# A hybrid decoder block on one core: raw weight tiles kept between the half turns of w_down, four segments, a start in 512-wide loads, and a new order

## The chip, the cores and the metric

The kernel runs on one core of a Trainium2 chip. The metric is the device time of one execution in microseconds (us); lower is better. The kernel before takes 1189.65 us, the median of 3 runs (1189.48 to 1189.77). The engines are TensorE (PE, matmuls), VectorE (DVE), ScalarE (ACT), GpSimd (POOL) and SyncE (SP, which issues the weight loads).

## The reference

One decoder block over 256 tokens of width 2048, all in float32: a modulation from a vector c, attention and a gated short convolution beside each other, an output projection, and a gated feed-forward network (FFN) with a convolution of three taps along the tokens. The change touches the FFN (h2 is the normalised, modulated x):

```
h2 = modulate(rms_norm(x, norm2_g[l]), sh2, sc2)
u = causal_dwconv(h2 @ w_ffn_up[l], ffn_conv_w[l], ffn_conv_b[l])
u_gate, u_up = jnp.split(u, 2, axis=-1)
ffn = (jax.nn.silu(u_gate) * u_up) @ w_ffn_down[l]
x = x + g2[:, None, :] * ffn
```

w_ffn_up is 2048 x 11264 and w_ffn_down is 5632 x 2048. The modulation also needs the gate g2, from c and the last 2048 columns of w_ada.

## The kernel before

**Slots.** The program is a row of 232 slots. A slot is one load of weights into a `raw` tile (128 x 2048 float32, 1 MB, six buffers), its split into two rounded halves, hi (ACT, line 341, `split_hi`) and lo (DVE, line 350, `split_lo`, raw minus hi), and PE's matmuls with both. Each product is made as hi x hi + hi x lo + lo x hi. When lo is made, the raw tile is free, and `load_next` issues the next load on SP's queue, in a fixed order. There are three hi and three lo tiles, and the split runs two slots ahead of PE (`la`). Slots 0 to 47 are the input projection, 48 to 63 the output projection, 64 to 231 the FFN.

**Up slots.** The 11264 columns of w_ffn_up are 44 units u of 256 columns; an even u is the gate's, an odd u the up part's, and units 2g and 2g + 1 make the 22 groups g. A unit has two slots of 8 x 128 rows each (`up_slot`, 32 matmuls, two banks of PSUM `z`). Slots 64 to 75 are the first halves of units 0 to 11. Their loads are 256 columns wide (1 KB rows). After a half, ACT copies and DVE adds the sums out of `z` into `ub` (lines 860 and 870). After the second half come the three taps: ACT scales (lines 890 and 892), and DVE adds (line 900), or POOL adds by an accumulating DMA (`dma_tap`, line 905, for the taps listed in `dma_taps`). Then silu, the product (line 915), and its halves gh and gl (lines 919 and 923).

**Down slots.** Groups 0 to 17 go through w_ffn_down by a scheme of seven products for a 2 x 2 block, in place of eight. The 2048 columns are two parts fp of 1024. For each group and part, an `r` slot makes three of the products from three of the four blocks of the raw tile (0.75 MB, two DMAs, lines 1038 and 1039), and a `T` slot the other four (1 MB, line 1035); ahead of a T slot's split, DVE makes sums of blocks in place (lines 360 and 363, `sums_of`). So each weight tile is loaded twice, three quarters of it the first time. The groups are cut into segments (`segs`: 4, 4, 4, 4, 2). In each segment, the `r` slots of a part are one turn and the `T` slots another; a turn adds up in three or four banks `q`, and at its end ACT copies them out (line 962) and POOL adds them to sums in DRAM by accumulating DMAs (line 964). At the end the sums are read back (`load_q`, line 978), joined on DVE (line 989, tiles l0.. for part 0 and l1.. for part 1), multiplied by g2 and added to x. Groups 18 to 21 follow directly, in the eight slots of the tail (224 to 231, banks `m('D', ...)`).

**Order.** The order of slots 76 to 223 on PE is the table `plan` ('0r1' is segment 0, r, part 1; a number is the next half of that unit). The order on the other engines comes from a planner in the program (from line 1623): a list of operations with costs, due times, tables of shifts and biases, and counts of free tiles. It picks operations one after another by its own clock. The chip then runs each engine's queue in that order, and an operation waits only for its data and buffers. The 16 tiles of w_ada for g2 are consumed on DVE between the slots (`g2at`).

Of the kernel before, what the change touches and what calls it, by code (L numbers as in the profile page):

```python
# [65 lines left out]
 'shift': {76: -5, 77: 1, 78: 9, 79: 10, 80: -3, 82: -6, 83: 1, 84: 6, 85: -2, 86: -3, 87: -9, 88: -14, 89: 5, 90: -7, 92:  # L66
# [18 lines left out]
 'bias': {'conv': -3, 'usa': 10, 'gate': 8, 'sum': 2, 'st': -47, 'lo': -27, 'ghi': -26, 'join': 3, 'glo': -3, 'evac': -3,  # L85
          'g2': 29, 'silu': 57},
# [6 lines left out]
 'segs': [4, 4, 4, 4, 2, 4],  # L93
 'join': [-70.0, -15],
 'tiles': 15,
 'early': 1.0,
 'spare': 4,
 'free0': 6,
 'spread': [[43, 0], [38, 1], [41, 1], [36, 1]],
# [19 lines left out]
 'gate': [41, 91, 23, 203],  # L119
# [48 lines left out]
 'direct': 2,  # L168
# [18 lines left out]
def tile_block(  # L187
# [108 lines left out]
    def arrive(issue):  # L296

        clock["DMA"] = max(clock["DMA"], clock["now"] + 1.5) + 2.7
        landed[issue] = clock["DMA"] + 1.5
# [29 lines left out]
    kind, held, ready_w = {}, {}, {}  # L329
# [17 lines left out]
    def split_lo(i=None):  # L347
        t, hi, nk, i = halfway.pop(0) if i is None else halves_of.pop(i)
        lo = half_tile("lo", i)
        V.tensor_tensor(out=lo[:, :nk], in0=t[:, :nk], in1=hi[:, :nk].bitcast(F32), op=ALU.subtract)  # L350
# [608 lines left out]
    def evac_q(seg, fp, n):  # L959
        if True:  # L960
            e = t2k(f"e{fp}{n}")
            act(e, qb.pop((seg, fp, n)), AF.Copy, scale=-1.0 if n in ("a", "c00", "c10") else 1.0)
# [68 lines left out]
    def down_load(k, f, nk):  # L1031
        def issue(t):
# [14 lines left out]
    def down_slot(seg, what, fp):  # L1047

        ga, gb = SEGS[seg]
        g = turn_at.get((seg, what, fp), ga)  # L1050
        turn_at[seg, what, fp] = g + 1
        first, last = g == ga, g == gb - 1
        assert g < gb
# [10 lines left out]
        i = len(slots)  # L1064
        kind[i], uses_g[i] = what, [g]
        nk = 3 if what == "r" else 4
        slots.append((down_load(2 * g, 2 * fp, nk), nk, go, 2.05 if what == "r" else 2.73, nk if first else 0))
# [3 lines left out]
    up_at = {}  # L1071

    def up_slot(u, one):
# [5 lines left out]
        def go(hi, lo):  # L1079
# [4 lines left out]
            if one:  # L1084
                for j, ft in order:
                    for w, v in ((hi, 0), (lo, 0), (hi, 1)):
                        mm(zp[u][ft][:, :256], w[:, j, ft * P:(ft + 1) * P], h2T[k + j][:, v * 256:v * 256 + 256],
                           start=begins and j == 0 and w is hi and not v, stop=ends and j == 7 and v == 1)
                return
# [18 lines left out]
        slots.append((up_load(u, k), 4, go, 5.76 if one else 5.55, 2 if begins else 0))  # L1108
        if ends:
            if i < F0 - 1:  # L1110
                at(i + 1, up_sum, u, one)
            else:
                ups.append((i, u, one, k == 8))

    def up_load(u, k):
        def issue(t):
            c = u % 2 * DFF + u // 2 * 256
            nc.sync.dma_start(t.rearrange("p a b -> p (a b)").rearrange("p (k f) -> p k f", k=8),
                              w_up[0, k * P:(k + 8) * P, c:c + 256].rearrange("(k p) f -> p k f", p=P))
        return issue  # L1120
# [9 lines left out]
    for u in range(NS):  # L1130
# [748 lines left out]
```

## Time and profile before

| | us |
|---|---|
| median of 3 runs | 1189.65 |
| profiled execution | 1195.88 |
| its span, first to last instruction | 1194.1 |
| mean granted PE clock in it | 0.985 |

The profiled execution is a single one and 6 us longer than the median of the runs; durations and waits below are taken from it. A row of a timeline gives the start, the length, the engine, line and operation, what it writes and reads, the number of instructions in it, and in brackets the idle time ahead of it and what ended that. A row of waits gives the waiting engine and line, what it waited for, then the total in us, the number of times and the longest. A row of groups gives the number of instructions, then busy time and mean ns of one, then idle time ahead of them.

### The profile page before, as it was taken

The page shows a single profiled execution, that of the slowest core. Times are in us where ns is not written, and L with a number is a line of the kernel's source. Part 1 is how long each engine was busy: PE and PEld are TensorE (multiplying, and loading weights), DVE is VectorE, ACT ScalarE, POOL GpSimd, SP SyncE. Part 2 cuts the span into 40 slices and gives each one's busy share as a digit, 9 for nine tenths or more (in the row PEclk, how much of TensorE's full clock was granted, in tenths as well). Part 3 has the DMA queues.
Part 4 walks back from the last instruction along what each step waited for, and adds up shares of the span by engine and source line. Part 5 has one row for each costly group of instructions (what it writes and reads, how often), then busy time and mean ns, then how long its engine had stood idle before and what let it go on. Part 6 is the DMA issues. An engine that isn't in the chain of part 4 may idle for free. (4 is left out here: it accounts for less than half of the span.)

```text
span 1194.1 us, 15939 instructions
## 1 busy us (share of the span) xinstructions
PE 1142.1 (96%) x5897; PEld 955.9 (80%) x5897; DVE 1062.7 (89%) x1153; ACT 781.4 (65%) x1187; POOL 116.7 (10%) x145
## 2 busy tenths in 40 slices
PE   7999999999999999799999999999999999997897
PEld 4767788888888888688888877878888787886776
DVE  4889989999999979899999989799999788985776
ACT  5644364668785554569886588577768776785641
POOL 2000000000000000002100011111011200131222
PEclk9999999999999999899999999999999999998899
DMA  9999989998798899899987999989889989999977
GB/s 364 408 412 390 410 333 388 378 375 313 281 331 309 292 363 335 298 307 312 306 267 271 323 347 318 312 262 336 287 259 283 311 274 307 294 265 272 305 216 144
DMA packets 205806, 374.86 MB, mean 314 GB/s; under 512 B 8464, under 2 KB 113636, under 8 KB 201376
## 3 DMA queue, kind: packets, MB, share of 16 engines
q1 hardware_dynamic: 185008, 339.63, 79.8%
q0 software_dynamic: 19280, 31.93, 13.9%
q10 hardware_dynamic: 1440, 2.29, 0.6%
q8 instruction: 46, 0.75, 0.2%
q14 instruction: 32, 0.26, 0.1%
HBM read 343.70 MB, written 23.59 MB: 308 GB/s over the span
## 5 line engine op out<-in xcount | busy, mean ns | idle before, releaser
L341 ACT ACTIVATE hi<-raw 128x2048 fp32r<-128x2048 f32 (+1 forms) x231 | 426.0, 1849 | 223.9 <-DMA raw<-in_w_in_dram 53.4
L350 DVE TENSOR_TENSOR lo<-raw,hi 128x2048 fp32r<-128x2048 f32 (+1 forms) x231 | 506.4, 2202 | 30.3 <-ACT hi L341 29.7
L1100 PE MATMUL z<-h,hi 128*128 128x512 f32 x1376 | 330.8, 393 | 7.3 <-DVE h L796 4.5
L1100 PEld LDWEIGHTS z<-h,hi 128*128 128x128 f32 x1376 | 256.0, 190 | 60.3 <-issue 4.9
L420 DVE SCALAR_TENSOR_TENSOR ada<-raw,csil,ada 128x512 f32<-128x512 f32 (+3 forms) x167 | 195.4, 1175 | 3.4
L1103 PEld LDWEIGHTS z<-h,lo 128*128 128x128 f32 x1376 | 178.0, 194 | 17.5 <-DVE lo L350 9.1
L1103 PE MATMUL z<-h,lo 128*128 128x256 f32 x1376 | 181.3, 286 | 9.3 <-DVE lo L350 7.2
L890 ACT ACTIVATE tap<-ub,fc 128x256 f32<-128x256 f32 x176 | 76.2, 501 | 3.5 <-DMA q<-e 3.3
L860 ACT ACTIVATE ub<-z 128x256 f32<-128x256 f32 x112 | 36.3, 376 | 51.6 <-PE z L1100 48.3
L360 DVE TENSOR_TENSOR raw<-raw 128x1024 f32<-128x1024 f32 x36 | 43.9, 1219 | 23.5 <-DMA raw<-in_w_ffn_down_dram 23.5
L892 ACT ACTIVATE uy<-ub,fc 128x256 f32<-128x256 f32 x88 | 47.9, 596 | 18.8 <-DVE ub L870 14.4
L1062 PE MATMUL qc<-lo,gh 128*128 128x512 f32 x108 | 43.0, 398 | 12.8 <-DVE lo L350 12.8
L363 DVE TENSOR_TENSOR raw<-raw 128x512 f32<-128x512 f32 x72 | 49.5, 690 | 1.8
L396 POOL MEMSET ada<- 128x2048 f32 x2 | 3.6, 1811 | 470.1 <-DVE lo L350 307.0
L900 DVE TENSOR_TENSOR uy<-tap,uy 128x508 f32<-128x508 f32 (+1 forms) x63 | 42.3, 684 | 7.3 <-DMA uy<-tap 5.8
L905 POOL DMA_DIRECT2D uy<-tap x25 | 30.1, 1206 | 171.9 <-ACT tap L890 107.6
L870 DVE TENSOR_TENSOR ub<-z,ub 128x256 f32<-128x256 f32 x108 | 40.5, 416 | 6.0 <-ACT ub L860 6.0
L1060 PE MATMUL qc<-hi,gl 128*128 128x512 f32 x108 | 42.2, 390 | 0.0
L1061 PE MATMUL qc<-hi,gh 128*128 128x512 f32 x108 | 42.2, 390 | 0.0
L1062 PEld LDWEIGHTS qc<-lo,gh 128*128 128x128 f32 x108 | 20.4, 189 | 19.4 <-DVE lo L350 15.4
L543 PE MATMUL mx<-hi,h 128*128 128x512 f32 x64 | 25.7, 401 | 1.2 <-ACT ada L466 1.2
L543 PE MATMUL mg<-hi,h 128*128 128x512 f32 x64 | 25.5, 399 | 0.0
(519 smaller groups left out, 1966.6 us busy)
## 6 DMA issues: line engine op xcount, KB each, us to landing
raw<-in_w_ada_dram SPq DMA_DIRECT2D x96, 1024.0 KB, 7.7
raw<-in_w_ffn_up_dram SPq DMA_DIRECT2D x88, 1024.0 KB, 8.0
raw<-in_w_in_dram SPq DMA_DIRECT2D x47, 1024.0 KB, 7.6
raw<-in_w_ffn_down_dram SPq DMA_DIRECT2D x44, 1024.0 KB, 8.0
raw<-in_w_ffn_down_dram SPq DMA_DIRECT2D x36, 512.0 KB, 5.6
raw<-in_w_out_dram SPq DMA_DIRECT2D x16, 1024.0 KB, 5.3
raw<-in_w_ffn_down_dram SPq DMA_DIRECT2D x36, 256.0 KB, 5.9
q<-e POOLq DMA_DIRECT2D x30, 256.0 KB, 8.9
```

Of the source, the lines that this page charges most:

```text
L341: act(hi[:, :nk], t[:, :nk], AF.Copy)
L350: V.tensor_tensor(out=lo[:, :nk], in0=t[:, :nk], in1=hi[:, :nk].bitcast(F32), op=ALU.subtract)
L360: V.tensor_tensor(out=t[:, 1::2], in0=t[:, 1:3], in1=t[:, 3:4].to_broadcast([P, 2, 512]), op=ALU.add)
L363: V.tensor_tensor(out=t[:, a], in0=t[:, a], in1=t[:, b], op=ALU.add)
L420: V.scalar_tensor_tensor(out=self.acc, in0=t[:, j, :], scalar=csil[:, i:i + 1], in1=self.acc, op0=ALU.mult, op1=ALU.add)
L543: mm(o, a, hi[:, k, s], start=(first and k == 0), stop=False)
L890: act(y, v, AF.Copy, scale=fcols[2 - d][:, i:i + 1])
L892: act(y, v, AF.Identity, bias=fcols[3][:, i:i + 1], scale=fcols[2][:, i:i + 1])
L900: V.tensor_tensor(out=pair(y)[:, :, d:], in0=pair(uz.pop((u, d)))[:, :, :256 - d], in1=pair(y)[:, :, d:], op=ALU.add)
L1062: mm(qb[seg, fp, n], x, lo[:, b], start=False, stop=last)
L1100: mm(zp[u][ft], hi[:, j, ft * P:(ft + 1) * P], h2T[k + j], start=begins and j == 0, stop=ends and j == 7)
L1103: mm(zp[u][ft][:, :256], lo[:, j, ft * P:(ft + 1) * P], h2T[k + j][:, :256], start=False, stop=False)
```

## The change

1. **Kept tiles.** `keep_raw` names, for each segment and part, how many of its last groups keep their raw tile between the r slot and the T slot: 2, 1, 3, 1, 2, 0, 0, 3, twelve in all. There, the r slot loads the whole tile in one DMA, and the T slot loads nothing; the raw buffer is not free until the T slot's lo is made. T turns run through their groups in falling order now.
2. **Segments.** Four (4, 4, 6, 4 groups) instead of five.
3. **Start.** Slots 64 to 75 take units in twos: a tile is 4 x 128 rows of 512 columns (2 KB rows), two units with the same g parity, and a pair of slots makes the first halves of both. Four banks are held over two slots instead of two over one.
4. **Order.** Another `plan`, `dma_taps`, `g2at`, and tables of shifts and biases; the planner's costs are changed. Its matmul slots that begin an up unit may have their lo 3.4 us late by its clock. One tap more is on DVE, and one fewer on POOL.

```diff
- 'segs': [4, 4, 4, 4, 2, 4],
- 'join': [-70.0, -15],
- 'tiles': 15,
+ 'segs': [4, 4, 6, 4, 4],
+ 'join': [-52.0, -203],
+ 'tiles': 16,
+ 'keep_raw': [2, 1, 3, 1, 2, 0, 0, 3],
...
-        load_next()
+        if i in keeps:
+            held[i] = t
+        else:
+            load_next()
...
-            held[i] = take(slots[i][0])
+            held[i] = held.pop(opener[i]) if i in opener else take(slots[i][0])
...
+        g = ga + n if what == "r" else gb - 1 - n
...
+        keep = g >= gb - CFG["keep_raw"][2 * seg + fp]
...
+        if keep and what == "r":
+            keeper[g, fp] = i
+            keeps.add(i)
+        elif keep:
+            opener[i] = keeper[g, fp]
+        slots.append((None if i in opener else down_load(2 * g, 2 * fp, 4 if keep else nk), nk, go, 2.05 if what == "r" else 2.73,
+                      nk if first else 0))
...
+    def start_slots(grp, one):
+        us = [4 * (grp // 2) + grp % 2 + w for w in (0, 2)]
+        for k in (0, 4):
+            def go(hi, lo, k=k):
...
+            slots.append((w_load(w_up, k, 4, [(grp % 2 * DFF + grp // 2 * 512, 512)]), 4, go,
+                          5.76 if one else 5.55, 4 if k == 0 else 0))
```

The first place is the end of SP's queue, from the last r loads to the tail. Lines 1038 and 1039 before (1041 and 1042 after) are the two DMAs of an r slot, 1035 (1038) a whole tile of w_down, 1118 (1161) an up load, 316 the tail's loads. Before:

```order
L1038 DMA raw<-in_w_ffn_down_dram 128x1024
L1039 DMA raw<-in_w_ffn_down_dram 128x512
L1038 DMA raw<-in_w_ffn_down_dram 128x1024
L1039 DMA raw<-in_w_ffn_down_dram 128x512
L1118 DMA raw<-in_w_ffn_up_dram 128x8x256 x3
L1035 DMA raw<-in_w_ffn_down_dram 128x2x1024
L1118 DMA raw<-in_w_ffn_up_dram 128x8x256
L1035 DMA raw<-in_w_ffn_down_dram 128x2x1024
L1118 DMA raw<-in_w_ffn_up_dram 128x8x256 x3
L1035 DMA raw<-in_w_ffn_down_dram 128x2x1024 x2
L1118 DMA raw<-in_w_ffn_up_dram 128x8x256
L316 DMA raw<-in_w_ffn_down_dram 128x4x512 x8
```

And after:

```order
L1041 DMA raw<-in_w_ffn_down_dram 128x1024
L1042 DMA raw<-in_w_ffn_down_dram 128x512
L1161 DMA raw<-in_w_ffn_up_dram 128x8x256
L1038 DMA raw<-in_w_ffn_down_dram 128x2x1024 x2
L1161 DMA raw<-in_w_ffn_up_dram 128x8x256 x2
L1038 DMA raw<-in_w_ffn_down_dram 128x2x1024
L1161 DMA raw<-in_w_ffn_up_dram 128x8x256 x4
L1038 DMA raw<-in_w_ffn_down_dram 128x2x1024 x4
L1161 DMA raw<-in_w_ffn_up_dram 128x8x256 x3
```

Before, every T slot has a load of its own (line 1035). After, the first whole tiles (x2) belong to the r slots 205 and 206, whose T slots load nothing; the single one after them is the only T load of part 1 in that segment, and the four (x4) are those of part 0, which keeps none there.

The second place is DVE's queue near slot 222, with the first join of part 1 (l1c, l), the lo of the next slots, and the gate's product and gl of groups 18 and 19. Before:

```order
L915 TENSOR_TENSOR uy_9284<-uy_9284,uy_9715 128x512
L350 TENSOR_TENSOR lo<-raw,hi 128x2048 x2
L923 TENSOR_TENSOR gl_9971<-uy_9284,gh_9964 128x512
L989 TENSOR_TENSOR l1c_9864<-l1c_9864,l1a 128x512
L989 TENSOR_TENSOR l_9862<-l_9862,l1a 128x512
L870 TENSOR_TENSOR ub_9989<-z_0_9669,ub_9989 128x256
L870 TENSOR_TENSOR ub_9989<-z_1_9670,ub_9989 128x256
L900 TENSOR_TENSOR uy_9910<-tap,uy_9910 128x2x254
L350 TENSOR_TENSOR lo<-raw,hi 128x2048
```

And after:

```order
L350 TENSOR_TENSOR lo<-raw,hi 128x2048
L992 TENSOR_TENSOR l1c_9594<-l1c_9594,l1a 128x512
L992 TENSOR_TENSOR l_9592<-l_9592,l1a 128x512
L350 TENSOR_TENSOR lo<-raw,hi 128x2048
L918 TENSOR_TENSOR uy_9162<-uy_9162,uy_9681 128x512
L350 TENSOR_TENSOR lo<-raw,hi 128x2048
L926 TENSOR_TENSOR gl_9940<-uy_9162,gh_9895 128x512
```

Before, the join stands behind the lo of slot 222, and part 1's last T slot is 217; after, it stands behind the lo of slot 221, and that T slot is 212.

The third place is DVE's queue at the join of part 0 (l0c, l), some ten rows later, with the ub and the taps of unit 43, the last. Before:

```order
L870 TENSOR_TENSOR ub_10124<-z_0_9869,ub_10124 128x256
L870 TENSOR_TENSOR ub_10124<-z_1_9870,ub_10124 128x256
L900 TENSOR_TENSOR uy_10003<-tap,uy_10003 128x2x254
L350 TENSOR_TENSOR lo<-raw,hi 128x2048
L900 TENSOR_TENSOR uy_10136<-tap,uy_10136 128x2x255
L900 TENSOR_TENSOR uy_10136<-tap,uy_10136 128x2x254
L989 TENSOR_TENSOR l0c_10087<-l0c_10087,l0a 128x512
L989 TENSOR_TENSOR l_10085<-l_10085,l0a 128x512
L350 TENSOR_TENSOR lo<-raw,hi 128x2048
```

And after:

```order
L350 TENSOR_TENSOR lo<-raw,hi 128x2048
L992 TENSOR_TENSOR l0c_9892<-l0c_9892,l0a 128x512
L992 TENSOR_TENSOR l_9890<-l_9890,l0a 128x512
L873 TENSOR_TENSOR ub_10037<-z_0_9901,ub_10037 128x256
L873 TENSOR_TENSOR ub_10037<-z_1_9902,ub_10037 128x256
L350 TENSOR_TENSOR lo<-raw,hi 128x2048
L903 TENSOR_TENSOR uy_10048<-tap,uy_10048 128x2x255
L903 TENSOR_TENSOR uy_10048<-tap,uy_10048 128x2x254
```

The join stood behind unit 43's ub and taps and ahead of the lo of slot 227, with part 0's last T slot at 222; now it stands ahead of unit 43's ub and of the lo of slot 226, with that T slot at 220.

More of the change, by code (lines that the diff above doesn't have):

```diff
@@ L296, in arrive @@
     def arrive(issue):
-        clock["DMA"] = max(clock["DMA"], clock["now"] + 1.5) + 2.7
+        clock["DMA"] = max(clock["DMA"], clock["now"] + 1.5) + getattr(issue, "us", 2.98)
         landed[issue] = clock["DMA"] + 1.5
@@ L1049, in down_slot @@
         ga, gb = SEGS[seg]
[L1050 to L1053, printed above, removed]
+        n = turn_at.get((seg, what, fp), 0)
+        turn_at[seg, what, fp] = n + 1
+        g = ga + n if what == "r" else gb - 1 - n
+        first, last = n == 0, n == gb - ga - 1
+        assert n < gb - ga
         def go(hi, lo):
@@ L1064, in down_slot, with up_slot @@
         i = len(slots)
+        keep = g >= gb - CFG["keep_raw"][2 * seg + fp]
         kind[i], uses_g[i] = what, [g]
         nk = 3 if what == "r" else 4
-        slots.append((down_load(2 * g, 2 * fp, nk), nk, go, 2.05 if what == "r" else 2.73, nk if first else 0))
+        if keep and what == "r":
[5 more added lines that the diff above has]
+                      nk if first else 0))
         if last:
             outs.extend((i, seg, fp, n) for n, *_ in FORM[what])
-    up_at = {}
-    def up_slot(u, one):
+    up_at, begin_at = {}, set()
+    def up_slot(u):
         k = up_at.get(u, 0)
@@ L1083, in go @@
             order = [(j, ft) for j in range(8) for ft in range(2)]
[L1084 to L1089, printed above, removed]
             wide = [e + (1,) for e in order]
@@ L1107, in up_slot @@
         up_slots.append((i, u))
-        slots.append((up_load(u, k), 4, go, 5.76 if one else 5.55, 2 if begins else 0))
+        if k == 0 and u >= NS:
+            begin_at.add(i)
+        slots.append((up_load(u, k), 4, go, 5.55, 2 if begins else 0))
         if ends:
+            ups.append((i, u, False, True))
+    def start_slots(grp, one):
+        us = [4 * (grp // 2) + grp % 2 + w for w in (0, 2)]
+        for k in (0, 4):
+            def go(hi, lo, k=k):
+                if k == 0:
+                    for u in us:
+                        zp[u] = [bank(f"z{u}_{ft}") for ft in range(2)]
+                z = zp[us[0]] + zp[us[1]] if us[0] in zp else None
+                parts = [(hi, 0), (lo, 0), (hi, 1)]
+                order = [(j, ft) for j in range(4) for ft in range(4)]
+                if one:
+                    run = [(0, ft, *e) for e in parts for ft in range(4)]
+                    run += [(j, ft, *e) for j in range(1, 4) for ft in range(4) for e in parts]
+                    for j, ft, w, v in run:
+                        mm(z[ft][:, :256], w[:, j, ft * P:(ft + 1) * P], h2T[k + j][:, v * 256:v * 256 + 256],
+                           start=k == 0 and j == 0 and w is hi and not v, stop=k == 4 and j == 3 and v == 1)
+                    return
+                wide = [e + (1,) for e in order]
+                low = [e + (0,) for e in order]
+                for j, ft, w in (wide + low if k == 0 else low + wide):
+                    if w:
+                        mm(z[ft], hi[:, j, ft * P:(ft + 1) * P], h2T[k + j], start=k == 0 and j == 0, stop=k == 4 and j == 3)
+                    else:
+                        mm(z[ft][:, :256], lo[:, j, ft * P:(ft + 1) * P], h2T[k + j][:, :256], start=False, stop=False)
+            i = len(slots)
+            slots.append((w_load(w_up, k, 4, [(grp % 2 * DFF + grp // 2 * 512, 512)]), 4, go,
+                          5.76 if one else 5.55, 4 if k == 0 else 0))
+        for u in us:
+            up_at[u] = 8
             if i < F0 - 1:
@@ L1129, in tile_block @@
     seven |= set(range(SEGS[-1][0]))
-    for u in range(NS):
-        up_slot(u, u < CFG["direct"])
+    for grp in range(NS // 2):
+        start_slots(grp, grp < CFG["direct"])
     for e in CFG["plan"]:
         if isinstance(e, int):
-            up_slot(e, False)
+            up_slot(e)
         else:
@@ L1137, in tile_block @@
     assert all(up_at[u] == 16 for u in range(44))
-    assert all(turn_at[n, w, fp] == SEGS[n][1] for n in range(len(SEGS) - 1) for w in "rT" for fp in range(2))
+    assert all(turn_at[n, w, fp] == SEGS[n][1] - SEGS[n][0] for n in range(len(SEGS) - 1) for w in "rT" for fp in range(2))
     LAST = len(slots)
@@ L1620, in tile_block, with __init__ @@
                 lo_of([j])
-    clock.update(PE=0.0, ACT=0.0, DVE=0.0, SP=0.0, POOL=0.0, DMA=0.0, now=0.0)
+    clock.update(PE=0.0, ACT=0.0, DVE=0.0, SP=0.0, POOL=0.0, DMA=8.0, now=0.0)
     ops = []
     class Op:
-        def __init__(self, e, cost, f, deps=(), due=1e9, need=(), free=(), lat=0.1, key=None, out=0, nb=0.0, tag=None, at=None):
+        def __init__(self, e, cost, f, deps=(), due=1e9, need=(), free=(), lat=0.1, key=None, out=0, nb=0.0, tag=None, at=None, soft=None):
             self.e, self.cost, self.f, self.deps, self.due = e, cost, f, [d for d in deps if d], due
@@ L1708, in tile_block @@
                 raw = None
[L1709 to L1710 removed]
+            hi_op[j] = Op("ACT", (1.41 if nk == 3 else 1.81 * nk / 4) + 0.02, lambda j=j: split_hi(slots[j][1], gated.get(j), j), d, key=raw, tag="hi", at=j)
+            lo_op[j] = Op("DVE", 1.79 if nk == 3 else 2.2 * nk / 4 + 0.01, lambda j=j: split_lo(j), [hi_op[j], pe.get(j - N_HL)], tag="lo", at=j)
         for g, r, *q in extra.get(i, []):
@@ L1733, in tile_block @@
                 free[q] = free.get(q, 0) + n
-        pe[i] = prev["pe"] = Op("PE", cost, lambda i=i: run_slot(i), d, due=tid[i + 1], need={"b": slots[i][4] + more}, free=free, lat=0.2)
+        soft = {}
+        if i in begin_at and lo_op.get(i):
+            soft[lo_op[i]] = 3.4
+            d.append(hi_op[i])
+        pe[i] = prev["pe"] = Op("PE", cost, lambda i=i: run_slot(i), d, due=tid[i + 1], need={"b": slots[i][4] + more}, free=free, lat=0.2, soft=soft)
         if more:
@@ L1823, in tile_block @@
                 continue
-            start = max([clock[o.e], o.nb] + [d.end + (0.05 if d.e != o.e else -1.0 if d.e == "PE" else 0.0) for d in o.deps] + [sorted(res[k])[n - 1] for k, n in o.need.items() if n]
+            start = max([clock[o.e], o.nb] + [d.end + (0.05 if d.e != o.e else -1.0 if d.e == "PE" else 0.0) - o.soft.get(d, 0.0) for d in o.deps] + [sorted(res[k])[n - 1] for k, n in o.need.items() if n]
                         + ([landed.get(o.key, 0.0)] if o.key is not None else []))
```

52 lines of the change are left out of this document (26 added, 26 removed), and 52 rows, old and new, of the table CFG.

## The prediction

> **What bounds the kernel now.** The page's busy shares come first, then the list of what TensorE (PE) waited for from 430 us on.
>
> ```profile
> PE 1142.1 (96%) x5897; PEld 955.9 (80%) x5897; DVE 1062.7 (89%) x1153; ACT 781.4 (65%) x1187; POOL 116.7 (10%) x145
> PE qc L1062 <- DVE lo L350: 12.8, 6, 8.0
> PE z L1103 <- DVE lo L350: 7.2, 4, 4.6
> PE z L1100 <- DVE h L796: 4.5, 1, 4.5
> PE z L1100 <- DVE ub L870: 2.6, 1, 2.6
> PE m('D', -1, 0)0_10094 L533 <- DVE gl L923: 2.3, 1, 2.3
> PE z L1103 <- ACT h L811: 2.1, 2, 1.6
> PE m('D', -1, 3)0_10339 L535 <- DVE lo L350: 1.7, 1, 1.7
> PE qa L1062 <- DVE lo L350: 1.2, 1, 1.2
> PE z L1100 <- ACT e1a L962: 0.2, 1, 0.2
> ```
>
> PE is busy for 96% of the span, and the order view has the same 5760 matmuls in both kernels. So the change can win back only what PE waits, and what its halved clock costs after a wait. The two waits for h (4.5 + 2.1) lie at slot 76, where the second half of h2 is made; that piece of the order stays. The other 28.0 us lie in the planned stretch and the tail. PE's timeline shows the larger ones:
>
> ```profile
> 718.90 1.30 PE L1100 MATMUL z<-h,hi 128*128 128x512 f32 x4 [2.65 <-DVE ub L870]
> 788.11 0.50 PE L1062 MATMUL qc<-lo,gh 128*128 128x512 f32 x1 [2.00 <-DVE lo L350]
> 954.01 2.18 PE L1103 MATMUL z<-h,lo 128*128 128x256 f32 x16 [2.16 <-DVE lo L350]
> 993.82 0.52 PE L1062 MATMUL qc<-lo,gh 128*128 128x512 f32 x1 [2.07 <-DVE lo L350]
> 1090.26 0.80 PE L1062 MATMUL qc<-lo,gh 128*128 128x512 f32 x1 [7.98 <-DVE lo L350]
> 1129.75 3.78 PE L1103 MATMUL z<-h,lo 128*128 128x256 f32 x16 [4.63 <-DVE lo L350]
> 1158.85 0.50 PE L533 MATMUL m('D', -1, 0)0_10094<-hi,gl 128*128 128x512 f32 x1 [2.27 <-DVE gl L923]
> 1180.57 0.50 PE L535 MATMUL m('D', -1, 3)0_10339<-lo,gh 128*128 128x512 f32 x1 [1.74 <-DVE lo L350]
> ```
>
> PE nearly always waits for VectorE (DVE), so the next view is what DVE waited for between 505 and 1150 us, with two rows of its timeline.
>
> ```profile
> DVE raw L360 <- DMA raw<-in_w_ffn_down_dram: 23.5, 7, 10.9
> DVE lo L350 <- ACT hi L341: 22.5, 26, 2.6
> DVE l0c L989 <- DMA l0c<-q0c: 6.4, 1, 6.4
> DVE uy L900 <- DMA uy<-tap: 5.8, 3, 4.1
> DVE l1c L989 <- DMA l1c<-q1c: 4.5, 1, 4.5
> 1086.78 1.23 DVE L360 TENSOR_TENSOR raw<-raw 128x1024 f32<-128x1024 f32 x1 [10.87 <-DMA raw<-in_w_ffn_down_dram]
> 1149.96 0.69 DVE L989 TENSOR_TENSOR l0c<-l0c,l0a 128x512 f32<-128x512 f32 x1 [6.43 <-DMA l0c<-q0c]
> ```
>
> This parts the 28.0 us into three. **A**, work: 5.2 us up to 770 us (the row at 718.90, the 1.2 for qa and six short ones), where DVE hardly idles but is behind. **B**, transfers: 2.00 + 2.16 + 2.07 + 7.98 = 14.2 us, where DVE stood for a load or a transfer just before; the 7.98 is the 10.87 us that DVE waited for one load of w_down. **C**, tail: 4.63 + 2.27 + 1.74 = 8.6 us, where DVE stood at the joins l1c and l0c with the next slots' lo queued behind.
>
> The windows add the clock (columns: PE, PEld, DVE, ACT, POOL busy, granted clock, DMA share, GB/s).
>
> ```profile
> 786.00:806.00 20.00, 18.00 (x88) 15.22 (x88) 19.00 (x18) 13.96 (x20) 3.56 (x5) 0.91 1.00 284
> 950.00:970.00 20.00, 17.84 (x94) 15.09 (x93) 18.04 (x23) 15.10 (x22) 0.00 (x0) 1.00 0.84 252
> 990.00:1010.00 20.00, 17.93 (x92) 15.14 (x91) 19.03 (x17) 12.32 (x17) 2.60 (x3) 0.91 1.05 321
> 1088.00:1104.00 16.00, 13.74 (x69) 11.85 (x70) 14.44 (x12) 11.62 (x13) 3.10 (x4) 0.84 0.87 261
> 1128.00:1148.00 20.00, 18.25 (x79) 15.69 (x80) 14.13 (x14) 13.84 (x22) 7.32 (x11) 0.85 0.97 291
> ```
>
> Missing clock times length gives 1.8 + 0 + 1.8 + 2.6 + 3.0 = 9.2 us; part of the last two falls on the wait itself, so I take 6 us. To be won at most: 28 + 6 = 34 us.
>
> The Trainium skill (TensorE: Matmul & The Clock Gate, "What's actually happening") has the clock halved after at least one idle window of about 3.4 us. The trace differs: a wait of 2.00 us was followed by a granted clock of 0.91, one of 2.16 us by 1.00. By that rule the 2 us waits would lose no clock, and those left over below would cost some 2 us less; the measured rows decide.
>
> **Transfers, part B.** The queues between 500 and 1190 us:
>
> ```profile
> q1 hardware_dynamic: 101569, 164.87, 69.5%
> q0 software_dynamic: 18815, 31.66, 24.0%
> ```
>
> Over 690 us, q1's 69.5% is 480 us for 164.87 MB, or 2.91 us per MB; q0's 24.0% is 166 us for 31.66 MB, or 5.23 us per MB. Where a tile is kept, its r slot loads 1.05 MB instead of 0.79 and its T slot nothing instead of 1.05: 0.79 MB fall away, over twelve tiles 9.4 MB, 27 us. One segment fewer takes away 2 x 7 evacuations, and one tap moves to DVE: 15 x 0.262 MB x 5.23 = 21 us. So 48 us of transfer time go. Slot by slot with these prices, slots 76 to 223 need 603 us of transfers before, against 596 us of PE: transfers are the longer of the two. After, they need 555 us and leave 41 us of room. Evacuations come where a turn closes: slots 188 to 222 hold eight closing turns before and five after. I take 14 of B's 14.2 us and its 4 us of clock as won. Bounds: nothing (the loads are late for another reason) and all 18.
>
> The 14 evacuations are off ACT too, 14 x 0.6 us, which ends no wait there.
>
> ```profile
> L962 ACT ACTIVATE e<-q 128x512 f32<-128x512 f32 x30 | 16.1, 595 | 0.1
> L350 DVE TENSOR_TENSOR lo<-raw,hi 128x2048 fp32r<-128x2048 f32 x118 | 268.5, 2286 | 19.6 <-ACT hi L341 19.3
> L363 DVE TENSOR_TENSOR raw<-raw 128x512 f32<-128x512 f32 x72 | 49.5, 690 | 1.8
> L360 DVE TENSOR_TENSOR raw<-raw 128x1024 f32<-128x1024 f32 x36 | 43.9, 1219 | 23.5 <-DMA raw<-in_w_ffn_down_dram 23.5
> ```
>
> **The order, part A.** DVE has one instruction more (a tap, 0.68 us). I gave each DVE row in program order its mean from the view by shape (three such rows above) and each slot PE's time (5.57, 2.05 and 2.74 us for up, r and T), and took DVE's sum up to a slot's lo minus PE's sum up to that slot. Counted from slot 74, DVE falls behind by up to 10 us before (slots 108 to 122; A's 1.23 lies at the beginning of them, its 2.65 just behind), and by at most 6 after; at slot 224 it is 21 us ahead before, and 13 after. So the early deficit is spread out. I take 4 of A's 5.2 us as won; bounds 0 and 5.2. The price: up to slot 224 DVE has 13 us to spare instead of 21, and each idle microsecond of DVE comes closer to PE.
>
> **The joins, part C.** Before, the l0 join needs its transfers 25.0 us after the last T slot (end 1124.96, join 1149.96), and the order gives it one up slot and three tail slots, 5.57 + 3 x 5.48 = 22.0. After, it stands behind three up slots and two tail slots, 27.7 us. The l1 join had 22.2 us, and has 39 now. The last lo stands ahead of the l0 gating now, which takes away the 1.74. But the ub of unit 43 now stands behind the l0 join, and with it the chain to the last gl, which PE needs 8 us later: if the join waits its 25 us, PE waits some 2 us for gl as before. I take 6 of 8.6 + 2 us; bounds 0 and 10.6.
>
> **The start, and the price of keeping.** Twelve up loads are 512 wide. The first twelve slots show no wait of PE for a transfer, so faster loads win nothing; their cover is that very slack. Four banks are held over two slots, and each group of four begins about 11 us after the group before the last has ended: 0, with a bound of 2 us lost. A kept tile takes one of six raw buffers until its T slot; one to three are out at a time. What a load needs is 8.0 us to land, 1.9 for hi and 2.3 for lo:
>
> ```profile
> raw<-in_w_ffn_up_dram SPq DMA_DIRECT2D x88, 1024.0 KB, 8.0
> L341 ACT ACTIVATE hi<-raw 128x2048 fp32r<-128x2048 f32 x117 | 223.5, 1915 | 96.0 <-DVE raw L363 30.8 <-PE z L1100 17.6 <-DVE raw L1808 15.4
> ```
>
> With three buffers left that is 12.2 / 3 = 4.1 us for a load, against (5.57 + 2.05) / 2 = 3.8 us of PE where up and r slots alternate: 0.3 us short in each. Three tiles are out in six slots, two in fifteen, where four buffers give 3.05 us. No row shows a stretch with three buffers; the bounds are 0 and the 7.98 of the worst load. I take 2, nearest to the 0.3 x 6.
>
> **Sum**: 14 + 4 + 6 - 2 = 22 us won of 34, from the profiled execution's own 1195.88 us (span 1194.1 and 1.8 around it). That gives 1173.9. The median of the runs is 1189.65, 0.9948 of it, so 1167.8, or 1168.
>
> **Rivals.** *All won* (0.10): A, B and C vanish and keeping costs nothing, 1195.9 - 34 = 1161.9, in the runs 1156. For: all three causes are eased at once. Against: DVE still has waits for ACT of 22.5 us, which nothing touches. *The waits move* (0.18): DVE has only 13 us to spare, so each late load or transfer comes through at another slot, and only C or B is won: 7 to 14 us, 1176 to 1183; with less than that it is within 0.2% (1187.3 to 1192.0, about what a measurement can tell from no change; 0.07 of the 0.18). That the tiles are not kept can't be: the order shows 12 T loads fewer. *Starved loads* (0.14, slower): SP issues in order, so one load that finds no free raw buffer holds up all behind it. One load before took far longer than 8.0 us; it is the one that DVE got at 1086.78:
>
> ```profile
> 1065.16 1.16 SPq L1035 DMA_DIRECT2D raw<-in_w_ffn_down_dram  x1
> ```
>
> If loads land in L us where tiles are out, the shortage is 6 x ((L + 4.2) / 3 - 3.8) + 15 x ((L + 4.2) / 4 - 3.8). At L = 16, between the two, it is 36 us instead of 2: 1195.9 - 24 + 36 = 1208, in the runs 1202. It decides from L = 14 on, where the shortage passes the 24 us won; its places are slots 127 to 133 and 205 to 209. For it: that load took 21.6 us with all six buffers in use. Against it: 48 us of transfers fewer.
>
> **How the numbers follow.** Forecast 1168 with 0.58, its own range 1160 to 1176. Faster: 0.58 + 0.10 + 0.11 = 0.79; same 0.07; slower 0.14. The range 1156 to 1188 leaves out about 0.04 below and 0.16 above.
>
> **What would show it.** Right: PE's waits after slot 76 near 10 us; no DVE wait for w_down above some 3 us; q0 near 28 MB and q1 9.4 MB less; joins without a wait over 2 us. Wrong: DVE waits for raw or SP waits for lo growing in slots 125 to 136, 160 to 167 or 200 to 211, where two or three tiles are kept; PE waits for ub in slots 66 to 76 (the banks); or waits of the old size spread over new slots.

## The result, and the profile after

The changed kernel takes 1172.74 us (median of 4 runs, 1171.35 to 1174.91); the kernel before took 1189.71 in the same comparison. The ratio is 0.9856 (95% interval 0.9836 to 0.9876): 17 us, or 1.4%, faster. The forecast was 1168, within 1156 to 1188.

The profiled execution of after took 1173.74 us, 1.0 more than its median; that of before had been 6.2 over its median. So the profiles differ by 22.1 us, the runs by 17. The busy shares of after, from its page, and the list of what PE waited for from 430 us on (total, times, longest):

```profile
PE 1132.9 (97%) x5897; PEld 951.1 (81%) x5897; DVE 1062.3 (91%) x1154; ACT 774.8 (66%) x1173; POOL 103.6 (9%) x130
```

```profile
PE qa L1067 <- DVE lo L350: 5.6, 2, 5.3
PE z L1109 <- ACT h L814: 3.3, 2, 2.4
PE z L1106 <- DVE ub L873: 2.8, 1, 2.8
PE z L1106 <- DVE h L799: 2.7, 1, 2.7
PE z L1109 <- DVE lo L350: 1.7, 2, 1.5
```

With two rows below 1 us the waits are 17.0 us, against 34.6 before. The two for h at slot 76 are 6.0 us of them, against 6.6 before. What lies behind slot 76 is 10.8 us instead of 28.0, and none of it is an old wait: PE's timeline has the larger ones at new places.

```profile
764.24 0.79 PE L1067 MATMUL qa<-lo,gh 128*128 128x512 f32 x1 [5.30 <-DVE lo L350]
849.89 0.50 PE L1106 MATMUL z<-h,hi 128*128 128x512 f32 x1 [2.75 <-DVE ub L873]
1049.51 2.18 PE L1109 MATMUL z<-h,lo 128*128 128x256 f32 x16 [1.48 <-DVE lo L350]
```

In the tail PE does not wait at all, although DVE still waits 6.9 us for q0c at the l0 join; its waits for w_down fell from 23.5 to 8.1 us (DVE's waits, 505 to 1150 us):

```profile
DVE raw L363 <- DMA raw<-in_w_ffn_down_dram: 8.1, 7, 4.2
DVE l0c L992 <- DMA l0c<-q0c: 6.9, 1, 6.9
```

Two things that were not in the sum show up. The first is the clock at slot 76. The windows (same columns as above) of before, and then of after:

```profile
497.00:512.00 15.00, 9.46 (x34) 7.89 (x35) 12.47 (x17) 7.08 (x15) 0.00 (x0) 0.66 0.64 195
```

```profile
497.00:512.00 15.00, 11.01 (x54) 9.32 (x55) 12.17 (x20) 9.34 (x15) 0.00 (x0) 0.89 0.62 218
```

Nearly the same waits, but in this execution a granted clock of 0.89 instead of 0.66: 15 x 0.23 = 3.5 us. Not all of it is the kernel's. The second execution of before has 0.66 again, but the other runs of the kernel after and its edits, with much the same waits there, have 0.77, and one of them (a_keep2) 0.66. The window of a_loads:

```profile
497.00:512.00 15.00, 11.87 (x52) 10.05 (x53) 12.17 (x19) 9.49 (x15) 0.00 (x0) 0.77 0.62 210
```

By that, 15 x 0.11 = 1.7 us are the usual gain, and the rest is luck of this execution. The second is the end. DVE's last row of before and of after:

```profile
1187.81 0.41 DVE L1010 TENSOR_TENSOR d<-m('D', -1, 3)2_10341,l 128x256 f32<-128x256 f32 x1
```

```profile
1162.18 0.41 DVE L1013 TENSOR_TENSOR d<-m('D', -1, 3)2_10248,l 128x256 f32<-128x256 f32 x1
```

Behind it, before ends at 1194.1, 5.9 us later, and after at 1172.0, 9.4 us later. PE and DVE gained 25.6 us, and the output's last transfers gave 3.5 of them back.

| us | before | after | difference |
|---|---|---|---|
| PE busy (the same 5760 matmuls) | 1142.1 | 1132.9 | -9.2 |
| PE's listed waits from 430 us on | 34.6 | 17.0 | -17.6 |
| end, behind DVE's last row | 5.9 | 9.4 | +3.5 |
| rest of the span | 11.5 | 12.7 | +1.2 |
| span | 1194.1 | 1172.0 | -22.1 |

PE's busy time, of the same matmuls, falls as the mean granted clock rises from 0.985 to 0.991.

### The profile page after: what moved, and what is told of

It reads as the page before. It is cut to its first block, busy times and chain, and to the rows that moved or that the text cites. A ratio compares the mean times of both kernels' runs of the same rounds, so it can differ in the third digit from the quotient of the medians.

```text
span 1172.0 us, 15818 instructions
## 1 busy us (share of the span) xinstructions
PE 1132.9 (97%) x5897; PEld 951.1 (81%) x5897; DVE 1062.3 (91%) x1154; ACT 774.8 (66%) x1173; POOL 103.6 (9%) x130
## 3 DMA queue, kind: packets, MB, share of 16 engines
q1 hardware_dynamic: 175408, 330.19, 79.0%
## 4 chain that ended last, share of the span: by engine, by line
PE 73%; DVE 9%; DMA 6%; issue 5%; ACT 3%; SPq 1%; POOL 1%; POOLq 0%; DVEq 0%; ACTq 0%
PE z L1106 20%; PE z L1109 10%; DMA raw<-in_w_ffn_up_dram 4%; DVE lo L350 4%; PE z L1144 3%; DVE ada L423 2%; PE q L1065 2%; PE q L1066 2%; PE q L1067 2%; DMA raw<-in_w_in_dram 2%; ACT hi L341 2%; PE z L1146 1%; PE qc L1067 1%; PE qc L1066 1%; PE qc L1065 1%
## 5 line engine op out<-in xcount | busy, mean ns | idle before, releaser
L1109 PEld LDWEIGHTS z<-h,lo 128*128 128x128 f32 x1216 | 154.7, 192 | 11.9 <-ACT h L814 3.7
L1109 PE MATMUL z<-h,lo 128*128 128x256 f32 x1216 | 157.7, 284 | 5.2 <-ACT h L814 3.3
```

The lines of the kernel that those rows point to most:

```text
L1109: mm(zp[u][ft][:, :256], lo[:, j, ft * P:(ft + 1) * P], h2T[k + j][:, :256], start=False, stop=False)
```

## Experiments

The question is which part of the change did it. Four theories: the **bytes** saved by the kept tiles; the **accumulating transfers** that the fifth segment needed; the **order**; and, for the new waits, the **raw buffers** that kept tiles hold. In the runs named b_ the kernel before is edited, in the others the kernel after. Ratios are to the kernel before in the same comparison; after itself has 0.9856. Before's median was 1189.71 us there and 1191.86 to 1193.16 in the later comparisons, so a difference of medians from two comparisons can be some 3 us off.

| run | median us | ratio | 95% interval |
|---|---|---|---|
| b_again, before once more | 1189.4 | (one run) | |
| b_noacc, without 56 accumulating DMAs | 1164.90 | 0.9754 | 0.9730 to 0.9777 |
| b_plain, the 56 as plain writes | 1165.83 | 0.9775 | 0.9744 to 0.9805 |
| b_evacs, without 14 of them | 1178.90 | 0.9878 | 0.9843 to 0.9913 |
| a_loads, 9.4 MB given back | 1172.96 | 0.9829 | 0.9804 to 0.9854 |
| a_evacs, 16 evacuation DMAs more | 1182.71 | 0.9907 | 0.9882 to 0.9931 |
| a_start, 1 KB rows at the start | 1171.71 | 0.9845 | 0.9811 to 0.9878 |
| a_keep2, one tile fewer kept | 1181.52 | 0.9908 | 0.9872 to 0.9944 |
| a_ada, two w_ada tiles moved | 1179.07 | 0.9888 | 0.9851 to 0.9925 |
| r_keep0, nothing kept, order of after | 1236.73 | 1.0390 | 1.0359 to 1.0421 |
| r_swap, two places of the order | 1170.42 | 0.9829 | 0.9802 to 0.9857 |
| r_all, the same and the end | 1169.14 | 0.9799 | 0.9776 to 0.9822 |

### How firm is the profile of before? (b_again)

No edit.

> The kernel before, profiled once more, unchanged. Its first profiled execution was 1195.88 us where the runs have a median of 1189.65. Theory one (the waits lie in the order): the same waits of PE at the same places, each within 0.3 us, 34.8 us from 430 us on. Theory two (some of them hang on when a transfer happens to land): the waits of part B differ by several us between the two executions, above all the 7.98 us one, and the profiled time is nearer to 1190.

PE's waits in this second execution:

```profile
PE qc L1062 <- DVE lo L350: 12.2, 5, 7.6
PE z L1100 <- DVE h L796: 4.5, 1, 4.5
PE z L1103 <- DVE lo L350: 4.1, 3, 3.8
PE m('D', -1, 0)0_10094 L533 <- DVE gl L923: 2.8, 1, 2.8
...
PE z L1100 <- DVE ub L870: 1.9, 1, 1.9
PE qa L1062 <- DVE lo L350: 0.4, 1, 0.4
```

Behind slot 76 that is 21.4 us instead of 28.0, and the time 1189.4. The large wait (7.55) and the two of 2 us before r slots are there again, but the 2.16 at 954 us and the last 1.74 are missing, and three more are smaller by 0.8 to 0.9 us. The second theory holds in part: the profiled execution had 6.6 us of waits that this one has not, but the largest wait is nearly the same in both. Which of the two is the usual one is open, as the seven runs of before in this comparison took 1190.71 to 1196.29 us.

### Are the accumulating transfers the cause of part B? (b_noacc, b_plain, b_evacs)

```diff
-                nc.gpsimd.dma_start(qd[fp, n], e, accum_op=ALU.add)
# b_plain, in its place:
+                nc.gpsimd.dma_start(dram.tile([P, 512], F32, name=f"y{seg}{fp}{n}"), e)
# b_evacs, in its place:
+                if n not in ("a", "c01") or (seg, n) == (2, "a"):
+                    nc.gpsimd.dma_start(qd[fp, n], e, accum_op=ALU.add)
```

> The kernel before without its 56 accumulating DMAs of the evacuations (the sums of segments 1 to 4 are left out of the result; ACT still copies them). 56 x 0.262 MB x 5.23 us per MB = 77 us of transfer time fewer, more than the 48 us that the change takes away; the order on PE, DVE, ACT and SP is that of before. Transfers as the cause of part B: its 14.2 us of waits and the 4 us of clock go, and the joins no longer wait for the last accumulations, so part C's 4.6 and 2.3 go too: 18 to 27 us faster, ratio 0.977 to 0.985. The old order as the cause: only the joins gain, 5 to 9 us, ratio 0.992 to 0.996.

> The kernel before with its 56 accumulating evacuation DMAs turned into plain writes of the same size, each to DRAM of its own that nobody reads (the sums of segments 1 to 4 are missing from the result). If it is the accumulation that is slow, nearly all of the 28 us of the run without them: ratio 0.975 to 0.981. If it is the number of the DMAs and their bytes: 4 to 14 us, ratio 0.988 to 0.997.

> The kernel before with 14 of its 56 accumulating evacuation DMAs left out (evacuations a and c01 of segments 1 to 4, all but a of segment 2; these sums are missing from the result), as many as the change takes away by its four segments; nothing else is moved. If the accumulating DMAs alone made the change's gain: 12 to 18 us faster, ratio 0.985 to 0.990. If each counts alike, 14 of 56 give a quarter of the 28 us that all 56 gave: 7 us, ratio 0.994. If the change's order did it: within 3 us, ratio 0.998 to 1.001.

Without the 56, before is 2.5% (28 us) faster, a little more than was expected and more than the change itself brings. Everything that PE still waits for behind slot 76 belongs to part A, 4.1 us in all (L1099 to L1102 stand one or two lines higher than in before):

```profile
PE z L1099 <- DVE ub L870: 1.9, 1, 1.9
PE qa L1061 <- DVE lo L350: 1.3, 1, 1.3
PE z L1099 <- ACT e1a L962: 0.7, 1, 0.7
PE z L1102 <- DVE lo L350: 0.2, 1, 0.2
```

As plain writes of the same size they cost nearly nothing: 0.9775. So it is not the number of the DMAs and not the bytes they carry. Part of the gain of both runs is C and not the price of a DMA: the joins no longer wait for the last sums (4.5 and 6.4 us of DVE in before; none in b_noacc, 1.9 at l0 in b_plain). POOL's queue (packets, MB, share of 16 engines' span) in b_again, b_noacc and b_plain:

```profile
q0 software_dynamic: 19280, 31.93, 13.9%
```

```profile
q0 software_dynamic: 11216, 17.25, 7.2%
```

```profile
q0 software_dynamic: 15696, 31.93, 10.2%
```

With spans of 1187.6, 1163.0 and 1164.2 us that is 165, 84 and 119 us: 81 / 56 = 1.45 us of all engines for an accumulating DMA of 0.262 MB, 35 / 56 = 0.63 for a plain one. Six of them and a tap are issued within 12 us (1063.6 to 1075.2) ahead of DVE's 10.87 us wait for a load, and so of PE's longest. The windows of before, ahead of that 7.98 us wait, and of b_plain at the same slots, some 10 us earlier (the last two columns are DMA share and GB/s):

```profile
1060.00:1070.00 10.00, 10.00 (x51) 8.51 (x50) 7.26 (x6) 7.46 (x10) 2.34 (x4) 1.00 1.09 318
1070.00:1080.00 10.00, 10.00 (x57) 8.73 (x57) 4.87 (x5) 6.99 (x12) 4.03 (x5) 1.00 1.09 295
```

```profile
1050.00:1060.00 10.00, 10.00 (x49) 8.40 (x48) 8.54 (x7) 9.71 (x12) 2.14 (x4) 1.00 1.06 384
1060.00:1070.00 10.00, 10.00 (x58) 8.81 (x58) 4.41 (x5) 7.28 (x11) 2.30 (x3) 1.00 1.07 371
```

The engines are full in both, but with accumulating DMAs they move 318 and 295 GB/s, with plain ones 384 and 371. This is what the loads lose there.

The run with 14 left out measures the dose that the change takes away: 14 us, 1.0 us for each, half of what all 56 bring. The first of the three cases holds. Part B is gone in it (the largest wait of PE between 725 and 1110 us is 0.44), while A and C stay:

```profile
720.24 5.34 PE L1101 MATMUL z<-h,hi 128*128 128x512 f32 x16 [2.42 <-DVE ub L870]
...
1113.49 0.79 PE L1104 MATMUL z<-h,lo 128*128 128x256 f32 x2 [5.20 <-DVE lo L350]
...
1142.74 0.51 PE L533 MATMUL m('D', -1, 0)0_10080<-hi,gl 128*128 128x512 f32 x1 [1.79 <-DVE gl L923]
```

### The same on the kernel after: bytes or accumulations? (a_loads, a_evacs)

```diff
# a_loads, where a kept tile's T slot begins:
+            if i in opener:
+                nc.sync.dma_start(dram.tile([P, 1536], F32, name=f"extra{i}"), w_down[0, :P, :1536])
# a_evacs, behind each evacuation (in segment 0 a plain write into the new dq):
+                if n in ("a", "c01"):
+                    nc.gpsimd.dma_start(dq[fp, n], e, accum_op=ALU.add)
```

> The kernel after, and for each of the twelve kept tiles a DMA of 0.79 MB on SP's queue at the T slot's place, from w_down to DRAM that nobody reads; nobody waits for it, and the order on all engines is that of after. It gives back the 9.4 MB that keeping saved, but no buffer is held or freed by it. Transfers as the cause: the saved transfers were worth some 18 x 27/48 = 10 us, so 1172.7 + 10 = 1183, ratio 0.994 (0.991 to 1.000). The new order as the cause: within 3 us of after, ratio 0.984 to 0.989.

> The kernel after with 16 more evacuation DMAs on POOL's queue, 0.262 MB each (12 of them accumulating), into DRAM that nobody reads: two more of the seven of each segment and part. It gives back about what the fifth segment cost, 16 x 1.37 = 22 us of transfer time. Transfers as the cause: 18 x 21/48 = 8 us, ratio about 0.992 (0.989 to 0.997). The new order as the cause: within 3 us of after, ratio 0.984 to 0.989.

The bytes cost nothing where this run puts them, at the beginnings of T slots. The load queue of a_loads, from its page, moves the 339.63 MB of before again, in 80.7% of 1170.5 us, where after needed 79.0% of 1172.0 (330.19 MB). That is 18.7 us more of all engines, and the two large waits are those of after to 0.03 us:

```profile
q1 hardware_dynamic: 177136, 339.63, 80.7%
```

```profile
765.96 0.79 PE L1069 MATMUL qa<-lo,gh 128*128 128x512 f32 x1 [5.27 <-DVE lo L350]
851.02 5.30 PE L1108 MATMUL z<-h,hi 128*128 128x512 f32 x15 [2.76 <-DVE ub L875]
```

The 16 evacuation DMAs, 4.2 MB, cost 10 us (1182.71 against a_loads' 1172.96 in the same comparison; 6 us by the ratio to after's 0.9856). One wait of PE is new, and the wait of 1.48 us that after has at 1049.51 has grown to 4.99:

```profile
630.94 3.34 PE L1111 MATMUL z<-h,hi 128*128 128x512 f32 x9 [2.86 <-ACT hi L341]
...
1059.31 3.63 PE L1114 MATMUL z<-h,lo 128*128 128x256 f32 x16 [4.99 <-DVE lo L350]
```

So the expectation of the bytes fell, and that of the accumulations held. The two large waits of after (5.27 and 5.14 at slot 135 in the two runs, 2.76 in both at slot 155) answer to neither of the two.

### The start (a_start)

```diff
-            slots.append((w_load(w_up, k, 4, [(grp % 2 * DFF + grp // 2 * 512, 512)]), 4, go,
+            def issue(t, k=k):
+                for h in range(2):
+                    c = grp % 2 * DFF + grp // 2 * 512 + h * 256
+                    nc.sync.dma_start(t[:, :, h * 256:h * 256 + 256], ...)
+            slots.append((issue, 4, go,
```

> The kernel after with the twelve loads of the start made in two DMAs each, 256 columns wide (1 KB rows) as before; tiles, banks and order as in after. The prediction's step: nothing, within 2 us of after, ratio 0.982 to 0.988. If the wider rows are worth something: slots 64 to 75 show waits for hi or lo, 3 us or more, ratio above 0.988.

1171.71 us, the same as after, and PE has no wait between 430 and 490 us in either.

The run shows one thing more. Its order behind the start is that of after, but at slot 155 the load landed some 2 us earlier by the kernel's own pace (the hi of that slot starts 3.6 us after the DVE row that stands ahead of its lo has ended, 5.4 in after), and the wait of 2.75 us is 0.48:

```profile
846.69 3.74 PE L1106 MATMUL z<-h,hi 128*128 128x512 f32 x15 [0.48 <-DVE ub L873]
```

So this wait can nearly vanish with no change of the order.

### The two new waits: buffers, w_ada or the order? (a_keep2, a_ada, r_keep0, r_swap)

At slot 135 (764 us) SP issued no load for 10 us; then DVE waited for the load of slot 137, with the lo of slot 135 queued behind it. SP's, ACT's and DVE's timelines of after:

```profile
736.63 0.34 SPq L391 DMA_DIRECT2D raw<-in_w_ada_dram  x1
747.19 0.34 SPq L1041 DMA_DIRECT2D raw<-in_w_ffn_down_dram  x1
...
749.45 0.38 SPq L1038 DMA_DIRECT2D raw<-in_w_ffn_down_dram  x1
```

```profile
753.40 1.49 ACT L341 ACTIVATE hi<-raw 128x1536 fp32r<-128x1536 f32 x1
```

```profile
759.84 1.23 DVE L363 TENSOR_TENSOR raw<-raw 128x1024 f32<-128x1024 f32 x1 [4.24 <-DMA raw<-in_w_ffn_down_dram]
...
762.43 3.95 DVE L350 TENSOR_TENSOR lo<-raw,hi 128x1536 fp32r<-128x1536 f32 x2
```

The hi of slot 135 was there at 754.9, so its lo could have been made then. Both a late load (749.45, landed ten us later) and the order are in it.

```diff
# a_keep2
- 'keep_raw': [2, 1, 3, 1, 2, 0, 0, 3],
+ 'keep_raw': [2, 1, 2, 1, 2, 0, 0, 3],
# a_ada
- 'g2at': [0, 0, 2, 5, 10, 12, 14, 33, 35, 46, 46, 54, 70, 72, 73, 76],
+ 'g2at': [0, 0, 2, 5, 10, 12, 14, 22, 28, 33, 35, 46, 46, 54, 70, 76],
# r_keep0, with the order of after written out as a list
+ 'keep_raw': [0, 0, 0, 0, 0, 0, 0, 0],
# r_swap, DVE's queue
+ lo of slot 135, lo of slot 136
  a tap, sums of slot 137
- lo of slot 135, lo of slot 136
...
+ ub of unit 23 (on ACT ahead of the hi of slot 155 as well)
  lo of slot 155, a tap
- ub of unit 23
```

> The kernel after with two kept tiles instead of three in segment 1, part 0; one load of 1 MB comes back and one raw buffer is free at slots 127 to 136. The planner orders the rest anew from slot 133 on. Buffers as the cause of the 5.3 us wait at slot 135 (764 us): it goes, with the 3.4 us of clock that it costs, and the last load before it is issued without the 10 us gap on SP's queue: 5 to 9 us faster than after, ratio 0.976 to 0.981. Transfers or the order as its cause: the wait stays within 2 us, ratio 0.983 to 0.988.

> The kernel after with two of the four w_ada tiles of slots 146 to 152 taken at slots 98 and 104 instead (with the planner's new order behind it). The w_ada tiles as the cause of the 2.75 us wait for ub at 850 us (each takes a raw buffer and 2.3 us of DVE): it goes with its clock, 3 to 5 us faster than after, ratio 0.979 to 0.983, unless the same shows at 660 to 700 us. Another cause: the wait stays, ratio 0.983 to 0.988.

> The kernel after without keeping: every r slot loads 0.75 MB and every T slot its whole tile, 9.4 MB more; nothing holds a raw buffer across the turns. The order of all engines is that of after, but for some twelve rows of DVE, where the first sums of a T slot go behind the next lo because their load is not issued yet. Transfers saved as the worth of keeping: 10 us slower than after, ratio 0.991 or more. Transfers that cost nothing, as the run with dummy loads showed, and a buffer that is not held: 0 to 9 us faster than after, ratio 0.976 to 0.984, the wait at slot 135 gone. A third case: keeping is what lets the sums be made early; then new waits of DVE for w_down at the T slots, and 3 us or more slower, ratio above 0.987.

> The kernel after with two places of its order changed and nothing else: at 755 us the lo of slots 135 and 136 goes ahead of a tap and of the sums of slot 137, which wait for their load; at 840 us the ub of unit 23 (ACT's copy and DVE's add) goes ahead of the hi and lo of slot 155, which wait for their load. If the order makes these two waits (5.3 and 2.75 us, and 5 us of clock behind them): the second goes whole, of the first some 3 us come back at slot 137, in all 5 to 9 us faster than after, ratio 0.976 to 0.981. If the late loads make them: the waits move to slots 137 and 155, within 2 us of after, ratio 0.982 to 0.988.

In a_keep2 the wait stays and a second one follows it; SP's gap is there as well (738.17 to 747.84), presumably since the load that came back takes up the buffer that was freed:

```profile
764.63 0.72 PE L1067 MATMUL qa<-lo,gh 128*128 128x512 f32 x1 [4.27 <-DVE lo L350]
772.41 0.79 PE L1067 MATMUL qc<-lo,gh 128*128 128x512 f32 x1 [3.60 <-DVE lo L350]
```

In a_ada the 2.75 us are gone, but the planner's new order has waits of its own (3.47 us at 771, 2.03 at 995), and its median is 6 us above that of after. Both ratios lie above all the ranges that were expected. Both runs say little about a cause, as the whole order behind the edit moved; they do say that a buffer or a w_ada tile fewer is no remedy by itself.

r_keep0 is the largest effect of all, 64 us slower than after, and the third case of its expectation. Its bytes are those of a_loads, which cost nothing; what is gone is the early start of the T slots. Each now needs a load in time, in an order that was made without those loads; what the some twelve moved rows of DVE add can't be told apart (DVE's waits; in the runs named r_ a list of the order stands in the file, and lines from there on lie 56 lower, so that L419 is 363 of after):

```profile
DVE raw L419 <- DMA raw<-in_w_ffn_down_dram: 68.4, 13, 11.5
```

In r_swap (L1121 and L1123 are 1065 and 1067 of after, L1162 is 1106) the wait of 5.30 became two at slot 137, whose load is the late one, and that of 2.75 one for the next unit's ub:

```profile
767.10 0.50 PE L1121 MATMUL qc<-hi,gl 128*128 128x512 f32 x1 [1.87 <-ACT hi L397]
769.42 0.79 PE L1123 MATMUL qc<-lo,gh 128*128 128x512 f32 x1 [1.59 <-DVE lo L406]
853.84 5.63 PE L1162 MATMUL z<-h,hi 128*128 128x512 f32 x16 [1.75 <-DVE ub L929]
```

5.30 to 3.46 and 2.75 to 1.75: about a third of each went. At slot 135 that is the order's, by all that the runs show: with after's order the wait was 5.30, 5.27, 5.14 and 4.71. At slot 155 it isn't shown, since the load landed earlier here too (hi 4.5 us behind the same row of DVE, 5.4 in after), and a_start had 0.48 there with after's order. What is left hangs on late loads, in the second case again by way of the order, for that ub is queued behind a hi that waited 1.2 us for its load. The run's median is 2.3 us below that of after, and the intervals overlap, so the expected 5 to 9 us are not there.

### The end (r_all)

DVE's last rows, beside the two places of r_swap:

```diff
+ L1080 l0c<-l0c,ada; l<-l,ada (their accumulating DMAs into the output follow on POOL)
  L1071, L1072 d<-m('D', -1, 2)..., d<-d,l1c, twice
- L1080 l0c<-l0c,ada; l<-l,ada
```

> The run with the two places of the order changed, and at the end of DVE's queue the last two products with g2 for part 0 (l0c and l, whose accumulating DMAs into the output follow) ahead of the last four sums of tail column 2, 2.6 us earlier. In after 9.4 us lie between the last row of DVE and the end of the span, in before 6.0. If these accumulating DMAs make the end: 2.5 us of it go, so 1167 to 1169 us where the run before had 1170.4, ratio 0.978 to 0.982. If the plain writes of column 2 or the last row's own writes make it: nothing, or 1 us lost, ratio 0.982 to 0.986.

DVE's last row now lies at

```profile
1160.95 0.41 DVE L1069 TENSOR_TENSOR d<-m('D', -1, 3)2_10248,l 128x256 f32<-128x256 f32 x1
```

and the span ends at 1169.0, 7.6 us behind it, where it was 9.4 in after: 1.8 of the expected 2.5 us. But this end differs between executions. With after's order at the end it was 8.2 in r_swap and 8.5 in a_loads and a_start, so only 0.5 to 0.9 us less than those are left, and the span is not shorter than r_swap's 1168.8. What did change is the chain that ended last: in after and r_swap it runs through POOL's DMAs of these two products (line 1028 of after), here, as in before, through DVE's last sums. The profiled execution was one of the longer ones of this kernel (1170.77); its five runs lie between 1165.35 and 1171.89. With a median of 1169.14 and a ratio of 0.9799 it is the fastest version here that computes the whole result. By the ratios it is 0.6% below after in its own comparison, and 0.3 to 0.5% below a_loads and a_start, which have the order of after; how much of that is real can't be told closer, and its interval overlaps that of r_swap.

## Why the prediction was right, step by step

**The base.** 22 us off the profiled 1195.88 gave 1173.9, and the profiled execution of after took 1173.74. The step that missed is the last: scaling this to the median with before's 0.9948. That factor stood for 6.6 us of waits in one execution of before (b_again). They were among the 28.0 that were to be won, so what was won of them is counted twice. After's own factor is 1172.74 / 1173.74 = 0.9991. This makes the 4.7 us between 1168 and 1172.7.

**The sum.** The terms that the prediction takes are 14 us of B's waits and 4 of its clock, 4 of A, 6 of C, less 2 for keeping: 26 us. Its sum has 14 + 4 + 6 - 2 = 22, with one of the two fours left out. With both it would have been 1169.9 for the profiled execution, 3.8 us below the measured 1173.74. So that the profile came out at 22 is luck, and luck also hides that several terms did not come out:

- **A, 4 us.** The waits went. They are in every run with the old order (3.2 us in b_again, 4.1 in b_noacc, 4.6 in b_evacs), and none is left at its place in after. That the order did it is argued: no run changes the order alone, and the new 5.30 us at 764 us lie in the same stretch.
- **B, 14 + 4 us.** The four waits went, and transfers were their cause, but the term was priced by the wrong measure. The prediction added up 48 us of transfer time, 27 for kept tiles and 21 for evacuations, against 603 us over all slots. The 27 us are worth nothing measurable (a_loads), and the 14 evacuations alone made 14 us (b_evacs). What tells the two apart is where they fall: the evacuations come in bursts where a turn closes and the engines are full, and there the accumulating kind takes 1.45 us where a plain one takes 0.63 (b_plain). The bursts are read from the one place at before's longest wait; no run spreads the same evacuations out.
- **Kept tiles, -2 us.** Too little, and for the wrong reason. The prediction counted six raw buffers; from slot 76 on one of them holds the sum for g2 (POOL's second memset of that tile, in after at 480.5 us), so that three tiles out leave two:

```profile
L399 POOL MEMSET ada<- x2: 1812/1814/1817, 174.1 to 480.5; 128x2048 f32 x2
```

  By the prediction's formula two buffers would give 12.2 / 2 - 3.8 = 2.3 us in each of six slots, 14 us. Measured are the 5.30 us at slot 135, in the stretch that was named, and its clock; a_keep2 shows that a tile fewer does not lift it. How much of it is the buffers' is open.
- **C, 6 us.** The 8.6 us of waits went whole. DVE still waits 6.9 us at the l0 join, but PE has enough work queued by then, and the 2 us for gl that were feared behind unit 43's ub did not come. That the earlier place of the join did it is read from the two traces; it was not tried alone. Given back is what the prediction passed over: the last products with g2 for part 0 now end 1.4 us before DVE does (5.3 in before), and the end is 3.5 us longer. Their transfers into the output are the likely cause, as the chain that ended last runs through them. The size is not firm: the end is 5.9 to 7.3 us in before and the runs named b_, 7.8 to 9.4 in those with after's end, and 7.6 in r_all.
- **Slot 76, "stays".** The waits stayed (6.0 us of 6.6), but the clock behind them gave 3.5 us in this execution, some 1.7 in most others, that were not in the sum.
- **Start, 0.** Right for the row size (a_start); the banks were not tried alone.
- **10 us of waits left.** 10.8 were measured, at places that were not foreseen. Of the signs that were named, these 10 us and the queues (q0 28.00 MB, q1 9.44 MB less) came; a DVE wait for w_down of 4.2 us, where at most some 3 were to be, and the l0 join's 6.9, where at most 2 were to be, speak against the account.

**The rivals.** *The waits move* came true in part: the 5.30, 2.75 and 1.48 us are new. *Starved loads* did not: tiles that are kept hold buffers, but DVE's waits for w_down fell to 8.1 us. r_keep0 shows the opposite danger, an order that needs the kept tiles. *All won* failed by these waits and the end.

Beside the 14 accumulating DMAs the rest of this large change (keeping, order, start) nets little: b_evacs has 0.9878 and after 0.9856, and the intervals overlap. By the traces it won A, C and some clock at slot 76, and paid with new waits, their clock, and the end; no run tests the order or the banks alone.

**The clock.** The Trainium skill (TensorE: Matmul & The Clock Gate, "What's actually happening") puts the halved clock behind at least one idle window of about 3.4 us. The runs here differ from it: in r_swap the row at 853.84 has 16 matmuls in 5.63 us behind a wait of 1.75, where the same 16 take 3.8 at full clock. The length of the wait alone doesn't decide: in before, the 16 matmuls behind the 2.65 us at 718.90 took 4.05.

## What to carry to other kernels

Do not add up transfer time over a long stretch and hold it against the engine's time: look for the places where the DMA share is at 1 and something waits, and take away what comes there in a burst. Price accumulating DMAs apart from plain ones, and ask whether fewer partial sums would do. A change that moves an engine's last work also moves the transfers behind it, so follow each output to where it lands; and before scaling a profiled sum to a median, profile the old kernel twice.

## What the hardware showed that was not expected

- An accumulating DMA of 0.262 MB took 1.45 us of all 16 engines and 144 packets in its queue's count, a plain write of the same size 0.63 us and 80 packets; and beside the first the engines moved 295 to 318 GB/s at full share, beside the second 371 to 384.
- 9.4 MB more on the load queue, 18.7 us of all engines, changed neither the time nor any large wait; no slot waited for them.
- After a wait of 1.75 us the clock was halved for some 3.7 us (16 matmuls took 1.84 us longer); behind nearly equal waits at slot 76 it was 0.54 or 0.66 over 15 us in the runs with the old start, and 0.66, 0.77 or 0.89 in those with the new one: steps of 0.11 to 0.12, which is 1.7 us of the 15.
